# A hybrid encoder block on one core: gate and up of the first feed-forward column side by side, and half of the first norm's sum of squares on GpSimd

## Chip, core and metric

The kernel runs on one core of one Trainium2 chip. The metric is device time in microseconds of that core. The kernel before takes 1099.4 us, the median of 3 runs (1099.27 to 1099.45).

A core has engines with an instruction queue each: TensorE (PE in the profile; PEld are its weight loads), VectorE (DVE), ScalarE (ACT), GpSimd (POOL) and SyncE (SP), which issues the DMA transfers. They run side by side and wait for one another by semaphores.

## What is computed

One layer over 528 tokens (16 learned meta tokens and 512 of the input) with 1024 features, in float32:

```python
h = h + 0.5 * swiglu(rms_norm(h, ffn1_norm), ffn1_gate, ffn1_up, ffn1_down)
u = rms_norm(h, mix_norm)
proj = u @ w_in
y_attn = diff_attention_mixer(proj[..., :ATTN_COLS], ...)
y_rwkv = rwkv7_mixer(proj[..., ATTN_COLS:], ...)
h = h + concatenate([y_attn, y_rwkv]) @ w_out
h = h + 0.5 * swiglu(rms_norm(h, ffn2_norm), ffn2_gate, ffn2_up, ffn2_down)
return h[:, N_META:]

def swiglu(x, w_gate, w_up, w_down):
    return (silu(x @ w_gate) * (x @ w_up)) @ w_down

def rms_norm(x, g):
    return x * rsqrt(mean(x * x, axis=-1) + 1e-6) * g
```

The change concerns the first line alone, and of it the first microseconds. The feed-forward has 2816 inner features.

## The kernel before

**Tiles.** Activations are held transposed: features on the 128 partitions, tokens along the free axis. `hT` is eight tiles `h` of 128 features x 528 tokens, and the gate and up weights of one column of 128 inner features come as one tile of 128 x (8 x 128) each. A product over 528 tokens is done in two halves of 264, each in a PSUM bank (`mm`, 8 banks in all).

**Three products for one.** Each float32 operand is split into a high and a low part in the type fp32r: the high part by a copy on ScalarE, the low part by a subtraction on VectorE. A product is then hi x hi + lo x hi + hi x lo, three matmuls for each of the 8 feature tiles and each half (`mm3`). The high and low parts of the tokens are called `hh` and `hl` for the first six tiles, `sh` and `sl` for the last two (which lie in the room of weights that come later); those of the weights `whi` and `wlo`. The token's gain of the norm is applied in the split; the factor 1/rms, which is one number for each token, is applied to the finished products.

**The first feed-forward (`ffn`).** It has 22 columns in five groups (`FSPLIT`). The first four columns (`PLAIN`) are done with `plain`: gate product, then up product, each over all 8 feature tiles, so 2 x 48 matmuls. The others are done with `seven`, which needs combinations of the tokens (`xh`, `xl`, `th`, `tl`) that `operands` makes on VectorE and ScalarE; the weights of `seven` are loaded into the tiles `wr`, with parts `ws`, `sh`, `sl`, `uh`, `ul`. After a group of columns, its share of the output is added into `h` by `down`, whose products (with `whi`, `wlo` of the down weights) are spread between the columns of the next group.

**The norm.** `norm_add` squares one token tile on ScalarE (`fd`) and adds it on VectorE to the sum `fc`; `norm_end` sums over the partitions with a matmul against ones (`mm<-fc,ones`) and makes `r`, which is 1/rms. Every column's finished product waits for `r`, and so do the operands of `seven`.

**What sets the order.** All instructions are first recorded; `Recorder.flush` (line 255) then puts them into order with a list scheduler. It uses an estimated cost of each instruction (`cost_of`, line 84), the buffers that are free, and a priority `nc.prio`; of what is ready on an engine, the smallest priority goes first. So every instruction has the same line in the profile, L506, and tiles are told apart by name. The order written so is the order in each engine's queue. Priorities that matter here: the tokens' loads from `FIRST` = -20 in steps of 2, quarters of the first weight tile between them (`PIECES` = (4, 1): gate of column 0 in four quarters of 128 KB, up whole), the norm's squares and adds `NORM` = 1 (behind other work), `operands` 2, everything else 0. Before the first token arrives, nine warming matmuls on `ones` run.

Of the kernel before, what the change touches and what calls it, by code (L numbers as in the profile page):

```python
# [10 lines left out]
F32 = mybir.dt.float32  # L11
# [500 lines left out]
class Build:  # L512
    FSPLIT, HBUF = (5, 5, 4, 4, 4), 8
    WARM = 9
    INHB, LATE, NORM, UBUF = 6, 2, 1, 1
    PLAIN, SEVENS, RAWS = (4, 5), 4, 3
    EARLY = (2, 4)
    FIRST = -20
    PIECES = (4, 1)
    GROUPS = ((4, 5, 6, 7), (0, 1, 2, 3))  # L520
# [40 lines left out]

    def wtile(self, src, n, k=None, pieces=1, first=0):
        nc = self.nc
        raw = self.wraw.tile([128, 8, 128], F32, name="wraw")
        if pieces > 1:
            hi = self.whl.tile([128, 8, 128], F32R, name="whi")
            lo = self.whl.tile([128, 8, 128], F32R, name="wlo", bufs=2)
            m = n // pieces
            for o in range(0, n, m):
                s = slice(o, o + m)  # L570
                nc.prio = first + 2 * o if first else 0
                nc.sync.dma_start(raw[:, s], src[:, s])
                nc.prio = 0
                nc.scalar.activation(hi[:, s], raw[:, s], AF.Copy)
                nc.vector.tensor_tensor(lo[:, s], raw[:, s], hi[:, s].bitcast(F32), op=ALU.subtract)
            return hi, lo
        nc.sync.dma_start(raw[:, 0:n] if k is None else raw[:, 0:n].rearrange("p (d k) c -> p d k c", k=k), src)
        hi = self.whl.tile([128, 8, 128], F32R, name="whi")
        lo = self.whl.tile([128, 8, 128], F32R, name="wlo", bufs=2)
        nc.scalar.activation(hi[:, 0:n], raw[:, 0:n], AF.Copy)  # L580
        nc.vector.tensor_tensor(lo[:, 0:n], raw[:, 0:n], hi[:, 0:n].bitcast(F32), op=ALU.subtract)
        return hi, lo

    def mm3(self, w, n, x, out, at=0):

        nc = self.nc
        hi, lo = (t[:, at:at + n] for t in w)
        for i in range(n):
            for u, v in ((hi, 0), (hi, 1), (lo, 0)):
# [31 lines left out]
    def norm_add(self, st, src):  # L621
# [9 lines left out]
        nc.prio = prio  # L631

    def norm_end(self, st, psum, out):
        nc = self.nc
# [13 lines left out]

    def ffn(self, gu, dn, xs, n, st, h, done, pools, pieces=(1, 1)):

# [3 lines left out]
        parts = [(0, HALF), (HALF, HALF)] if n == L else [(0, n)]  # L654
        norm, r, gain = st
        self.norm_end(norm, psum, r)
        plain, before = self.PLAIN[n == MAIN], []
        f0 = 0
        for si, cnt in enumerate(self.FSPLIT):
            hs = []  # L660
            for i in range(cnt):
# [5 lines left out]
                if f < plain:  # L667
                    a = self.plain(gu, f, xs, r, n, parts, tp, pieces)
                else:
                    a = self.seven(gu, f, T, n, tp, sp, 3 if f < plain + self.LATE else 0)  # L670
# [19 lines left out]

    def plain(self, gu, f, xs, r, n, parts, tp, pieces):
        nc, psum = self.nc, self.pmm
        ps = []
        for g in range(2):
            w = self.wtile(gu[f, :, g], KT, pieces=1 if f else pieces[g], first=0 if f or g else self.FIRST + 1)
            pg = [psum.tile([128, 512], F32, name="mm") for _ in parts]
            self.mm3(w, KT, xs, [(o, m, p) for (o, m), p in zip(parts, pg)])
            ps.append(pg)
# [137 lines left out]
    def layer(self, ffn1=True, mixer=True, ffn2=True):  # L836
# [16 lines left out]
        with ExitStack() as ph:  # L853
# [16 lines left out]
            if ffn1:  # L870
# [3 lines left out]
                st = self.norm_begin(tp, L)  # L874
                for k in range(KT):
                    self.norm_add(st, hT[k])
                r1 = hp.tile([128, L], F32, name="r1")
                self.ffn(A["gu1"], A["dn1"], xs, L, (st, r1, lambda k: self.v("n1", k)), hT, done, (tp, hb, sp), self.PIECES)
# [741 lines left out]
```

## Time and profile before

| | before |
|---|---|
| median of 3 runs | 1099.4 us (1099.27 to 1099.45) |
| the profiled execution | 1091.92 us, its span 1090.1 us |
| TensorE busy | 1075.3 us, 99% of the span |
| VectorE busy | 834.7 us, 77% |
| ScalarE busy | 530.4 us, 49% |
| GpSimd busy | 10.1 us, 1%, 46 instructions |
| first token tile in use | matmuls on it from 5.29 us |
| TensorE without a gap | from 13.30 us for 96.75 us |

The span is the stretch from the first to the last recorded instruction of one profiled execution. A busy TensorE here is one that has a matmul in its pipeline; consecutive matmuls overlap, so the distance from one start to the next is shorter than the duration shown. The chain of waits follows the last instruction back to what released each step, and so shows which engine or transfer sets the end at each time. In a timeline row, `x2` means two instructions of the same kind, put together.

### The profile page before, as it was taken

The page shows a single profiled execution, that of the slowest core. Times are in us where ns is not written, and L with a number is a line of the kernel's source. Part 1 is how long each engine was busy: PE and PEld are TensorE (multiplying, and loading weights), DVE is VectorE, ACT ScalarE, POOL GpSimd, SP SyncE. Part 2 cuts the span into 40 slices and gives each one's busy share as a digit, 9 for nine tenths or more (in the row PEclk, how much of TensorE's full clock was granted, in tenths as well). Part 3 has the DMA queues.
Part 4 walks back from the last instruction along what each step waited for, and adds up shares of the span by engine and source line. Part 5 has one row for each costly group of instructions (what it writes and reads, how often), then busy time and mean ns, then how long its engine had stood idle before and what let it go on. Part 6 is the DMA issues. An engine that isn't in the chain of part 4 may idle for free.

```text
span 1090.1 us, 21488 instructions
## 1 busy us (share of the span) xinstructions
PE 1075.3 (99%) x8580; PEld 990.2 (91%) x8580; DVE 834.7 (77%) x1664; ACT 530.4 (49%) x945; POOL 10.1 (1%) x46
## 2 busy tenths in 40 slices
PE   8999999999999999999999999999999999999998
PEld 8999999999999998878888888688899999999996
DVE  7999786878875766887785657679978877777853
ACT  7554443433432654584576377646544443444421
POOL 0000000000000100000000000000000000000000
PEclk9999999999999999999999999999999999999999
DMA  7324324233221534434153222143233233233214
GB/s 241 116 63 134 106 72 127 72 103 113 76 64 46 193 116 110 115 99 115 51 140 80 69 80 78 59 156 121 96 93 108 91 107 112 68 116 117 68 30 135
DMA packets 75428, 110.57 MB, mean 101 GB/s; under 512 B 39488, under 2 KB 41024, under 8 KB 75328
## 3 DMA queue, kind: packets, MB, share of 16 engines
q1 hardware_dynamic: 75328, 109.19, 32.8%
q8 instruction: 68, 1.11, 0.4%
q14 instruction: 32, 0.26, 0.1%
HBM read 97.94 MB, written 10.04 MB: 99 GB/s over the span
## 4 chain that ended last, share of the span: by engine, by line
PE 89%; DVE 5%; ACT 2%; SPq 2%; DMA 1%; issue 1%; ACTq 0%; DVEq 0%
PE mm L506 89%; SPq L506 2%; DVE e L506 1%; DVE wlo L506 1%; DVE Tm L506 1%; DMA gd<-e 1%; DVE pr L506 1%; ACT e L506 0%; DMA h<-in_hT_dram 0%; DVE Zd L506 0%; DMA ad<-e 0%; ACT whi L506 0%; DVE n L506 0%; DVE xl L506 0%; DVE kb L506 0%
## 5 line engine op out<-in xcount | busy, mean ns | idle before, releaser
L506 ACT ACTIVATE whi<-wraw 128x1024 fp32r<-128x1024 f32 (+3 forms) x135 | 109.5, 811 | 167.2 <-PE mm L506 127.3
L506 PE MATMUL mm<-hh,wlo 128*128 128x264 f32 (+1 forms) x684 | 183.7, 322 | 1.3 <-DVE wlo L506 1.3
L506 PE MATMUL mm<-hl,whi 128*128 128x264 f32 (+1 forms) x684 | 184.3, 323 | 0.6 <-DVE hl L506 0.5
L506 PE MATMUL mm<-hh,whi 128*128 128x264 f32 (+1 forms) x684 | 184.2, 322 | 0.1
L506 PE MATMUL mm<-xl,sh 128*128 128x264 f32 (+1 forms) x490 | 138.5, 283 | 0.0
L506 PE MATMUL mm<-xh,sl 128*128 128x264 f32 (+1 forms) x490 | 138.5, 283 | 0.0
L506 PE MATMUL mm<-xh,sh 128*128 128x264 f32 (+1 forms) x490 | 138.1, 282 | 0.0
L506 ACT ACTIVATE sh<-ws 128x1024 fp32r<-128x1024 f32 x70 | 74.1, 1060 | 121.3 <-PE mm L506 116.2
L506 DVE TENSOR_TENSOR wlo<-wraw,whi 128x1024 fp32r<-128x1024 f32 (+3 forms) x135 | 122.7, 909 | 4.4 <-ACT whi L506 4.3
L506 PEld LDWEIGHTS mm<-hh,wlo 128*128 128x128 f32 x684 | 114.1, 189 | 11.0 <-DVE wlo L506 1.5
L506 PEld LDWEIGHTS mm<-hl,whi 128*128 128x128 f32 x684 | 114.3, 189 | 10.1 <-DVE hl L506 1.4
L506 PEld LDWEIGHTS mm<-hh,whi 128*128 128x128 f32 x684 | 114.4, 189 | 9.7 <-ACT hh L506 0.4
L506 PE MATMUL mm<-xh,whi 128*128 128x264 f32 (+1 forms) x448 | 114.4, 316 | 1.5 <-ACT whi L506 0.7
L506 PE MATMUL mm<-xh,wlo 128*128 128x264 f32 (+1 forms) x448 | 113.8, 315 | 1.4 <-DVE wlo L506 1.4
L506 PE MATMUL mm<-xl,whi 128*128 128x264 f32 (+1 forms) x448 | 112.5, 314 | 0.0
L506 PE MATMUL mm<-tl,sh 128*128 128x264 f32 (+1 forms) x350 | 99.0, 283 | 0.0
L506 PE MATMUL mm<-th,sl 128*128 128x264 f32 (+1 forms) x350 | 99.0, 283 | 0.0
L506 PE MATMUL mm<-th,sh 128*128 128x264 f32 (+1 forms) x350 | 98.9, 283 | 0.0
L506 DVE TENSOR_TENSOR sl<-ws,sh 128x1024 fp32r<-128x1024 f32 x70 | 85.5, 1222 | 16.4 <-ACT sh L506 16.4
L506 PEld LDWEIGHTS mm<-xh,sh 128*128 128x128 f32 x490 | 92.4, 189 | 0.8
L506 PEld LDWEIGHTS mm<-xl,sh 128*128 128x128 f32 x490 | 92.4, 189 | 0.7
L506 PEld LDWEIGHTS mm<-xh,sl 128*128 128x128 f32 x490 | 92.3, 188 | 0.0
(281 smaller groups left out, 2134.0 us busy)
## 6 DMA issues: line engine op xcount, KB each, us to landing
wr<-in_gu_dram SPq DMA_DIRECT2D x70, 512.0 KB, 4.1
wraw<-in_wi_dram SPq DMA_DIRECT2D x26, 512.0 KB, 3.6
wraw<-in_dn_dram SPq DMA_DIRECT2D x48, 256.0 KB, 2.7
wraw<-in_dn_dram SPq DMA_DIRECT2D x32, 320.0 KB, 3.0
wraw<-in_gu_dram SPq DMA_DIRECT2D x17, 512.0 KB, 3.7
wraw<-in_wo_dram SPq DMA_DIRECT2D x8, 512.0 KB, 4.0
h<-in_hT_dram SPq DMA_DIRECT2D x8, 264.0 KB, 4.9
h1d<-h SPq DMA_DIRECT2D x8, 264.0 KB, 2.1
```

The source lines that it names most:

```text
L506: ins = o.fn(*map(real, o.a), **{k: real(v) for k, v in o.k.items()})
```

## The change

The four constants: `PIECES` is 4 for (4, 1), and `NORM` -1 for 1. Three pieces of code:

- `begin` (new) issues the start of the first feed-forward. The gate and up weights of column 0 both come in four quarters, between the token tiles, and for each token tile the matmuls of gate and those of up follow each other. Behind them come the weights and products of the gate of column 1, whose weights (and those of its up) are put into the room of the weights of `seven` (`room=sp`).
- `norm_side` (new) squares the first four token tiles on GpSimd, each as a product of the tile with itself, and adds them up there: four products and three sums. VectorE and ScalarE do the other four tiles as before, and one more addition on VectorE takes GpSimd's sum `fb` into `fc`.
- `plain` uses what `begin` has made for columns 0 and 1.

With `NORM` at -1 the squares and adds of all three norms are ahead of work of priority 0, the two later norms' too.

```diff
-    INHB, LATE, NORM, UBUF = 6, 2, 1, 1
+    INHB, LATE, NORM, UBUF = 6, 2, -1, 1
-    PIECES = (4, 1)
+    PIECES = 4
...
-    def wtile(self, src, n, k=None, pieces=1, first=0):
+    def wtile(self, src, n, k=None, pieces=1, first=0, room=None):
         nc = self.nc
+        if room:
+            raw = room.tile([128, 8, 128], F32, name="wr", bufs=self.RAWS)
+            hi, lo = (room.tile([128, 8, 128], F32R, name=x) for x in ("sh", "sl"))
+            nc.sync.dma_start(raw, src)
+            nc.scalar.activation(hi, raw, AF.Copy)
+            nc.vector.tensor_tensor(lo, raw, hi.bitcast(F32), op=ALU.subtract)
+            return hi, lo
...
-    def mm3(self, w, n, x, out, at=0):
+    def mm3(self, w, n, x, out, at=0, only=None):
...
-        for i in range(n):
+        for i in range(n) if only is None else (only,):
...
+    def norm_side(self, pool, srcs):
+        nc = self.nc
+        acc = pool.tile(list(srcs[0].shape), F32, name="fb")
+        nc.gpsimd.tensor_tensor(acc, srcs[0], srcs[0], op=ALU.mult)
+        for x in srcs[1:]:
+            sq = pool.tile(list(x.shape), F32, name="fa")
+            nc.gpsimd.tensor_tensor(sq, x, x, op=ALU.mult)
+            nc.gpsimd.tensor_tensor(acc, acc, sq, op=ALU.add)
+        return acc
...
+        self.begun = {}
+        if pieces > 1:
+            self.begin(gu, xs, parts, sp, pieces)
         self.norm_end(norm, psum, r)
...
+    def begin(self, gu, xs, parts, sp, pieces):
+        ws = [self.wtile(gu[0, :, g], KT, pieces=pieces, first=self.FIRST + 1) for g in range(2)]
+        ps = [[self.pmm.tile([128, 512], F32, name="mm") for _ in parts] for _ in range(2)]
+        for i in range(KT):
+            for w, pg in zip(ws, ps):
+                self.mm3(w, KT, xs, [(o, m, p) for (o, m), p in zip(parts, pg)], only=i)
+        w = self.wtile(gu[1, :, 0], KT, room=sp)
+        pg = [self.pmm.tile([128, 512], F32, name="mm") for _ in parts]
+        self.mm3(w, KT, xs, [(o, m, p) for (o, m), p in zip(parts, pg)])
+        self.begun = {0: ps, 1: [pg]}
+
+    def plain(self, gu, f, xs, r, n, parts, tp, sp, pieces):
         nc, psum = self.nc, self.pmm
-        ps = []
-        for g in range(2):
-            w = self.wtile(gu[f, :, g], KT, pieces=1 if f else pieces[g], first=0 if f or g else self.FIRST + 1)
+        ps = self.begun.pop(f, [])
+        for g in range(len(ps), 2):
+            w = self.wtile(gu[f, :, g], KT, room=sp if f == 1 and pieces > 1 else None)
...
-                for k in range(KT):
+                side = self.norm_side(tp, hT[:4])
+                for k in range(4, KT):
                     self.norm_add(st, hT[k])
+                nc.prio = self.NORM
+                nc.vector.tensor_tensor(st["acc"], st["acc"], side, op=ALU.add)
+                nc.prio = 0
```

What moves in the order of the instructions, at the places that the prediction speaks of. First SyncE, the start of the program; `h` are token tiles, `wraw_105` the gate's and `wraw_106` the up's weights of column 0 (- before, + after):

```order
 L506 DMA h_94<-in_hT_dram 128x528
 L506 DMA wraw_105<-in_gu_dram 128x256
-L506 DMA h_109<-in_hT_dram 128x528
-L506 DMA h_112<-in_hT_dram 128x528
+L506 DMA wraw_106<-in_gu_dram 128x256
+L506 DMA h_111<-in_hT_dram 128x528
+L506 DMA h_115<-in_hT_dram 128x528
 L506 DMA wraw_105<-in_gu_dram 128x256
-L506 DMA h_118<-in_hT_dram 128x528
-L506 DMA h_130<-in_hT_dram 128x528
+L506 DMA wraw_106<-in_gu_dram 128x256
+L506 DMA h_134<-in_hT_dram 128x528
```

A quarter of up's weights now stands behind each quarter of gate's, ahead of token tiles that were ahead of it; before, up came whole behind the last token.

On GpSimd nothing stood here before. After the change its queue has this behind the constants' MEMSETs of the start; `fb_129` is its sum, `fa` a square:

```order
L506 ISA
L506 TENSOR_TENSOR fb_129<-h_94 128x528
L506 TENSOR_TENSOR fa_159<-h_111 128x528
L506 TENSOR_TENSOR fa_160<-h_115 128x528
L506 TENSOR_TENSOR fb_129<-fb_129,fa_159 128x528
L506 TENSOR_TENSOR fa_159<-h_134 128x528
L506 TENSOR_TENSOR fb_129<-fb_129,fa_160 128x528
L506 TENSOR_TENSOR fb_129<-fb_129,fa_159 128x528
```

The ISA row is an instruction that the compiler puts ahead of the first arithmetic of this kind on GpSimd.

On VectorE, behind the splits of the first tokens, before (rows 14 to 21 of its order); `fc_147<-fc_147,fd_185` is an add of the norm, `sl_217` the low part of the last token:

```order
L506 TENSOR_TENSOR fc_147<-fc_147,fd_185 128x528
L506 SCALAR_TENSOR_TENSOR sl_217<-h_169,vec_87,sh_208 128x528
L506 TENSOR_TENSOR wlo_155<-wraw_106,whi_135 128x1024
L506 TENSOR_TENSOR fc_147<-fc_147,fd_185 128x528
L506 TENSOR_TENSOR sl_218<-wr_178,sh_209 128x1024
L506 TENSOR_TENSOR fc_147<-fc_147,fd_185 128x528
L506 TENSOR_TENSOR sl_219<-wr_179,sh_210 128x1024
L506 TENSOR_TENSOR fc_147<-fc_147,fd_185 128x528
```

And after (rows 16 to 24), where `fc_207` is the norm's sum, `fb_129` GpSimd's, and `sl_271` and what follows are weights of column 1 and of `seven`:

```order
L506 SCALAR_TENSOR_TENSOR sl_270<-h_183,vec_87,sh_253 128x528
L506 TENSOR_TENSOR fc_207<-fc_207,fd_237 128x528
L506 SCALAR_TENSOR_TENSOR sl_270<-h_204,vec_87,sh_253 128x528
L506 TENSOR_TENSOR wlo_155<-wraw_105,whi_136 128x256
L506 TENSOR_TENSOR fc_207<-fc_207,fd_237 128x528
L506 TENSOR_TENSOR wlo_156<-wraw_106,whi_137 128x256
L506 TENSOR_TENSOR fc_207<-fc_207,fb_129 128x528
L506 TENSOR_TENSOR sl_271<-wr_214,sh_254 128x1024
L506 TENSOR_TENSOR sl_272<-wr_215,sh_255 128x1024
```

The adds of the norm now stand between the splits of the last tokens instead of behind them, there are fewer of them, and the last one, row 22, reads GpSimd's sum; all VectorE work of the later columns is behind it.

On TensorE, at the first matmul that reads the last operand `tl` (before: `tl_719`, row 440; rows 434 to 442 are shown):

```order
L506 MATMUL mm_102<-tl_717,sh_211 128x264
L506 MATMUL mm_102<-th_685,sl_220 128x264
L506 MATMUL mm_96<-xh_460,sh_208 128x264
L506 MATMUL mm_96<-xl_512,sh_208 128x264
L506 MATMUL mm_101<-xh_459,uh_264 128x264
L506 MATMUL mm_101<-xl_511,uh_264 128x264
L506 MATMUL mm_98<-tl_719,sh_210 128x264
L506 MATMUL mm_98<-th_687,sl_219 128x264
L506 MATMUL mm_101<-xh_459,ul_421 128x264
```

After, six matmuls of `down` (`hh_126` and `hh_127` with the down weights `whi_136`, `wlo_155`) stand at rows 437 to 442, between the products of the sevens:

```order
L506 MATMUL mm_103<-tl_783,uh_388 128x264
L506 MATMUL mm_96<-tl_784,sh_254 128x264
L506 MATMUL mm_96<-th_749,sl_271 128x264
L506 MATMUL mm_103<-th_748,ul_466 128x264
L506 MATMUL mm_97<-hh_126,whi_136 128x264
L506 MATMUL mm_97<-hl_145,whi_136 128x264
L506 MATMUL mm_97<-hh_126,wlo_155 128x264
L506 MATMUL mm_97<-hh_127,whi_136 128x264
L506 MATMUL mm_97<-hl_146,whi_136 128x264
L506 MATMUL mm_97<-hh_127,wlo_155 128x264
```

and the first matmul on the last operand, here `tl_787`, is row 471 (rows 467 to 472 are shown):

```order
L506 MATMUL mm_98<-th_751,sl_270 128x264
L506 MATMUL mm_100<-tl_785,sh_255 128x264
L506 MATMUL mm_100<-th_750,sl_272 128x264
L506 MATMUL mm_102<-xh_527,sl_270 128x264
L506 MATMUL mm_96<-tl_787,sh_254 128x264
L506 MATMUL mm_96<-th_752,sl_271 128x264
```

Up to that matmul TensorE's queue now has 31 more matmuls than before.

## Rows read from the trace of the kernel before

**Rows 1.** The page's first line of engines: busy us, share of the span, instructions

```profile
PE 1075.3 (99%) x8580; PEld 990.2 (91%) x8580; DVE 834.7 (77%) x1664; ACT 530.4 (49%) x945; POOL 10.1 (1%) x46
```

**Rows 2.** Chain that ended last, 0 to 110 us: start us, us, what

```profile
3.54 5.04 DMA h<-in_hT_dram
...
9.37 0.57 DVE hl L506
...
12.91 0.35 DVE wlo L506
...
13.30 96.75 PE mm L506 x771
```

**Rows 3.** Windows: stretch, length, busy (PE, PEld, DVE, ACT, POOL), clock, DMA, GB/s

```profile
0.00:20.00 20.00, 16.87 (x88) 15.11 (x89) 13.86 (x24) 15.77 (x25) 0.20 (x4) 0.91 0.86 294
...
80.00:100.00 20.00, 20.00 (x166) 20.00 (x165) 19.63 (x34) 10.93 (x16) 0.00 (x0) 1.00 0.32 108
sum 100.00, PE 96.87 PEld 94.57 DVE 93.32 ACT 59.53 POOL 0.20; mean PE 19.37 PEld 18.91 DVE 18.66 ACT 11.91 POOL 0.04
...
13.60:17.05 3.45, 3.45 (x18) 3.45 (x17) 3.45 (x5) 3.02 (x4) 0.00 (x0) 0.51 1.01 411
```

**Rows 4.** In time, at 66 us: start us, us, engine, line, operation, out<-in

```profile
65.11 0.70 DVE L506 TENSOR_TENSOR tl<-fb,th 128x528 fp32r<-128x528 f32 x1
...
66.00 0.28 PE L506 MATMUL mm<-tl,sh 128*128 128x264 f32 x1
```

**Rows 5.** In time on PE, in the first column, after it, norm sum

```profile
13.65 0.64 PE L506 MATMUL mm<-hh,whi 128*128 128x264 f32 x2
...
14.09 0.64 PE L506 MATMUL mm<-hl,whi 128*128 128x264 f32 x2
...
22.98 0.41 PE L506 MATMUL mm<-sh,wlo 128*128 128x264 f32 x2
...
23.22 0.41 PE L506 MATMUL mm<-hh,whi 128*128 128x264 f32 x2
...
24.45 1.16 PE L506 MATMUL mm<-fc,ones 128*128 128x264 f32 x4
```

**Rows 6.** In time: a DMA's issue on SP, the last token on ACT

```profile
1.64 0.43 SPq L506 DMA_DIRECT2D wraw<-in_gu_dram  x1
...
12.80 0.72 ACT L506 ACTIVATE sh<-h,vec 128x528 fp32r<-128x528 f32 x1
```

**Rows 7.** In time on DVE: splits, adds and sums of each shape

```profile
4.78 0.77 DVE L506 SCALAR_TENSOR_TENSOR hl<-h,vec,hh 128x528 fp32r<-128x528 f32 x1 [3.69 <-ACT hh L506]
...
12.83 0.76 DVE L506 TENSOR_TENSOR wlo<-wraw,whi 128x256 fp32r<-128x256 f32 x2
...
22.48 0.69 DVE L506 TENSOR_TENSOR ws<-ws,wr 128x512 f32<-128x512 f32 x1
...
24.31 1.22 DVE L506 TENSOR_TENSOR wlo<-wraw,whi 128x1024 fp32r<-128x1024 f32 x1
...
40.56 0.70 DVE L506 TENSOR_TENSOR xl<-fd,xh 128x528 fp32r<-128x528 f32 x1
41.17 0.70 DVE L506 TENSOR_TENSOR xl<-fb,xh 128x528 fp32r<-128x528 f32 x1
```

**Rows 8.** Groups on POOL by shape: busy us, mean ns, idle before

```profile
L506 POOL MEMSET O<- 128x1024 f32 x2 | 1.9, 957 | 12.7 <-PE mm L506 12.7
...
L506 POOL MEMSET vm<- 128x128 f32 x4 | 0.8, 205 | 475.5 <-PE mm L506 475.5
```

**Rows 9.** In time: the two COPYs on POOL and DVE beside them

```profile
385.56 0.76 DVE L506 SCALAR_TENSOR_TENSOR e<-praw,vec,e 128x528 f32<-128x528 f32 x1
...
385.95 0.42 POOL L506 COPY Mz<-eye 64x16 f32<-64x16 f32 x1 [4.62 <-DMA eye<-in_eye_dram]
...
471.40 1.22 DVE L506 TENSOR_TENSOR wlo<-wraw,whi 128x1024 fp32r<-128x1024 f32 x1
...
472.48 0.19 POOL L506 COPY Mz<-eye 64x16 f32<-64x16 f32 x1 [5.47 <-DMA zm<-Mz]
```

More of the change, by code (lines that the diff above doesn't have):

```diff
@@ L646, in norm_end, with ffn @@
             nc.vector.scalar_tensor_tensor(y, t, -3.0, y, op0=ALU.add, op1=ALU.mult)
-    def ffn(self, gu, dn, xs, n, st, h, done, pools, pieces=(1, 1)):
+    def ffn(self, gu, dn, xs, n, st, h, done, pools, pieces=1):
         nc, psum = self.nc, self.pmm
@@ L667, in ffn @@
                 if f < plain:
-                    a = self.plain(gu, f, xs, r, n, parts, tp, pieces)
+                    a = self.plain(gu, f, xs, r, n, parts, tp, sp, pieces)
                 else:
@@ L689, in down @@
             done(d)
-    def plain(self, gu, f, xs, r, n, parts, tp, pieces):
+    def begin(self, gu, xs, parts, sp, pieces):
[9 more added lines that the diff above has]
+    def plain(self, gu, f, xs, r, n, parts, tp, sp, pieces):
         nc, psum = self.nc, self.pmm
-        ps = []
-        for g in range(2):
-            w = self.wtile(gu[f, :, g], KT, pieces=1 if f else pieces[g], first=0 if f or g else self.FIRST + 1)
+        ps = self.begun.pop(f, [])
+        for g in range(len(ps), 2):
+            w = self.wtile(gu[f, :, g], KT, room=sp if f == 1 and pieces > 1 else None)
             pg = [psum.tile([128, 512], F32, name="mm") for _ in parts]
```

## Prediction

> **What bounds the kernel now.** I read the page first, then the chain of waits, then the windows of the first 120 us, and last the order in time on each engine around the places that these point to. TensorE is busy for 99% of the span, VectorE for 77%, GpSimd for 1% [rows 1]: whatever makes TensorE late or early by a microsecond moves the end by that microsecond. The chain shows where it is not yet so: up to 13.30 us it runs through the loads of the token tiles and their splits, and from there 96.75 us long through matmuls alone [rows 2]. The start of the first feed-forward is therefore the only place that this change can win at. The windows show the second thing: from 20 to 100 us TensorE is busy all the time, but VectorE too (93.32 of 100 us, and at least 19.63 of each 20 us from 20 on) [rows 3]. Its work is a chain of its own: the last operand of the first seven-product column (`tl`, of `operands`) starts on VectorE at 65.11 and takes 0.70, and the matmul that reads it starts at 66.00, 0.19 later [rows 4]. So at 66 us there is no slack between the two engines. A TensorE that is earlier is worth something only if VectorE is at 66 us not later.
>
> **What the change gives TensorE.** Before, only the gate product can run while the tokens come in; up runs after it and ends at 23.2 [rows 5]. After, both run on each token tile, 12 matmuls a tile. The four added DMAs bring up's 512 KB ahead of the last token instead of behind it. At the 294 GB/s of the first 20 us [rows 3] that is 1.8 us, and the last token's high half, at 12.80 before [rows 6], begins at about 14.5. SP issues them between others, 0.43 us each [rows 6], and nothing but these loads stands behind them. The split then needs 0.72 on ScalarE and 0.76 on VectorE [rows 6, 7], so 16.0; one add and two splits of weight quarters follow (0.62 + 2 x 0.35): 17.3. With the last eight matmuls TensorE has both products at about 18.3, against 23.2: 4.9 us ahead. A pair of matmuls takes 0.24 [rows 5], so 0.122 each.
>
> **What it asks of VectorE.** I count instructions in the order up to the last `tl`, and price them by the distance from one start to the next, which in a full queue is some 0.08 below the duration: 0.62 for 128x528 with two tensors, 0.68 with a gain, 0.35 for 128x256 (a pair of them takes 0.76), 0.61 for 128x512, 1.14 for 128x1024 [rows 7]. Before there are 104. After there are 106: four more of 128x256 (+1.4), three fewer adds of the norm (-1.9), one more of 128x512 (+0.6). So 58.7 us before and 58.8 after: no relief. What counts is when VectorE is through with the start, which ends with the new add of GpSimd's sum (`fc += fb`, row 22 of its order). I call its end T. Up to there VectorE has 8 x 0.68 + 8 x 0.35 + 4 x 0.62 = 10.8 us of work from 4.78 [rows 7] on. With the waits for the tokens it is through at T = 18.0 if GpSimd costs nothing: the 17.3 above and the add. That holds 18.0 - 4.8 - 10.8 = 2.4 us of waits. From T to the end of the last `tl` there are 86 instructions, 48.1 us, and 0.3 of small waits as before: T + 48.4.
>
> **The sum.** At the last `tl` the order of TensorE stands 31 matmuls further on than before (row 471 against 440), because matmuls of `down` fill in: 31 x 0.122 = 3.8 us of work already done. Before, that place is at 66.0; after, it is at T + 48.4 + 0.2. So the change of the time is T + 48.6 - 66.0 - 3.8 = **T - 21.2**. With T = 18.0 that is -3.2. (TensorE itself, from 18.3 through 370 matmuls at 0.122 and two halves of the norm's sum at 0.58 [rows 5], would be there at 64.6, so VectorE decides, and 1.7 us of the 4.9 are lost there.) What remains after it is the same work on both engines. At two earlier points I looked for a cost and found cover: TensorE runs at 1.2 GHz from 13.6 to 17.05 after idling [rows 3]; a pair there takes 0.44 [rows 5], so if it happens again TensorE loses at most 3.45 / 2 = 1.7 us, which the 2.0 us by which it waits at the last `tl` hold. The weights of the second column go to the room of the seven-product weights, whose next loads come later; their splits are in the count of 106. The earlier priority of the two later norms (-1 for 1) moves ScalarE and VectorE work where TensorE is busy and VectorE is not full: nothing.
>
> **What GpSimd does to T.** It gets seven instructions of 128x528, four squares and three sums, each with two inputs in SBUF. The trace has none of that kind, so I bound one from its MEMSETs and COPYs [rows 8]: 205 ns for 128 columns and 957 for 1024 make 0.84 ns a column and pass. One pass over 528 is 0.54 us; a fixed part of the shorter COPY (0.19) with two passes is 1.08, with three 1.52. I take 1.2, just above the two passes that two inputs need, so 8.4 us in all (3.8 to 10.6).
>
> Whether these run beside VectorE decides the case. The one thing the trace shows: a COPY of 64x16 on GpSimd takes 0.19 us at 472.48, where VectorE's big subtraction is just ending. The same COPY takes 0.42 at 385.95, where VectorE is in the middle of a 128x528 instruction with two SBUF tensors (385.56 + 0.76 = 386.32), and it ends at 386.37, right behind it [rows 9]. The reader on GpSimd seems to have been held until VectorE's instruction was over. In the start nearly all of VectorE's work is of this form. If the two take turns, T is moved by GpSimd's 8.4 us less what falls into VectorE's 2.4 us of waits. I take half of them, 1.2, since the tokens that end VectorE's waits start GpSimd as well: T = 18.0 + 8.4 - 1.2 = 25.2, and **+4.0 us: 1103.4**. It does not matter which one holds the other: what GpSimd has not done when VectorE reaches the add, VectorE waits for there. The ends are 3.8 - 2.4 (T = 19.4, -1.8) and 10.6 - 0 (T = 28.6, +7.4).
>
> The Trainium skill ("SBUF — State Buffer", section "Who interferes with whom") says the same as a rule, and it speaks against this change: a VectorE instruction with two SBUF inputs and a GpSimd instruction that reads SBUF exclude each other for the whole instruction, and the one issued second is blocked. The COPY of 0.42 us agrees. By the rule T is 25.2, without it 18.0.
>
> The Trainium skill ("GPSIMD Engine Reference", section "Elementwise — side-by-side cycle accounting") gives 4497 ns for such an addition of 2048 columns; scaled to 528 an estimate is 1.16 us, which would make the sum 1103.1. No run here shows it yet.
>
> **The rivals.**
> *Side by side.* GpSimd takes its sums from arrival to arrival and never holds VectorE; its last one ends before 17.3. Then T = 18.0 and the time is 1099.4 - 3.2 = 1096.2. For it: before, the fourth token was being split at 9.37 [rows 2]; with three weight quarters more ahead of it that is about 10.7, and the square and the sum that follow end at 13.1. Against it: the COPY of 0.42. It decides from T below 21.2 on.
> *Side by side, but late.* The order puts one more instruction, an ISA, on GpSimd ahead of its first square; the trace of before has no such row, so it may cost nothing or many microseconds. If the first square starts at s, GpSimd ends at s + 8.4 and T = s + 9.0. Break-even is s = 12.2; s between 10 and 14.4 makes -2.2 to +2.2, around 1099.4. Against it: GpSimd is busy for 0.20 of the first 20 us [rows 3], so the load would have to last 10 us.
> The Trainium skill ("GPSIMD Engine Reference", section "Instruction dispatch") gives about 6 us for the first call of a freshly loaded kernel. From 0.7 this would be s = 6.7, and T would still be 18.0; it would also take GpSimd out of VectorE's early waits, where the two take turns.
>
> **How the numbers follow.** Taking turns 0.58, side by side 0.24, side by side but late 0.18. The likeliest gives 1103.4, by itself 1100 to 1106.5. The sums are shifts against the profiled execution (1091.92, span 1090.1), which stands 7.5 below the median of the runs, 1099.4; I add them to the median. What a measurement of this kernel tells from no change is about 0.2%, 2.2 us, so 1097.2 and 1101.6 are the borders. Of the 0.58, 0.53 is above 1101.6, 0.04 between, 0.01 below; of the 0.24, 0.21 below and 0.03 between; of the 0.18, 0.13 between, 0.03 above, 0.02 below. Faster 0.24, same 0.20, slower 0.56. The range goes from 1096.2, the middle of the side by side case, to 1106.0; about 0.12 and 0.05 are left outside.
>
> **What would show it.** In the profile after: VectorE instructions of 128x528 and 128x256 between 5 and 25 us that are longer than 0.70 and 0.42, or idle ahead of them that ends with GpSimd; GpSimd instructions well over 1.2 us; `fc<-fc,fb` ending near 25 and waiting for GpSimd; the last `tl` near 73 and a wait of TensorE for it. I am wrong if `fc<-fc,fb` ends before 21: then the rest of the sum gives a gain. The sum itself is wrong if T is as I say and the last `tl` is not 48.4 behind it, or if a new wait of TensorE shows up after 75 us.

## Result, and the profile after

| | before | after |
|---|---|---|
| median of 5 runs | 1099.27 us (1097.7 to 1099.45) | 1104.62 us (1103.78 to 1105.47) |
| ratio | | 1.0052, 95% interval 1.0037 to 1.0066 |
| matmuls in the first 200 us of the profiled execution | 1558 | 1514 |
| end of the last `tl` | 65.81 us | 74.07 us |

The kernel became 5.35 us slower; the forecast was 1103.4, by taking turns. The two profiled executions, 1091.92 and 1105.47 us, are not subtracted here: most runs of the kernel before take 1098 to 1102 us and a few 1091 to 1093, at a granted clock that late in the span is a little higher, and the profiled one is such a run. So times are compared by medians, and the start by the number of matmuls done in the first 200 us, at 0.122 us each.

The profile after, first the windows of the profiled execution (stretch; length, busy us and count of PE, PEld, DVE, ACT, POOL; granted clock; DMA share; GB/s). They answer to [rows 3]; 22.38 is where the prediction's T now lies:

```profile
0.00:20.00 20.00, 15.37 (x92) 13.48 (x92) 13.80 (x20) 11.25 (x22) 9.80 (x11) 1.00 0.72 242
20.00:40.00 20.00, 18.18 (x133) 17.70 (x132) 17.95 (x30) 12.76 (x18) 0.00 (x0) 0.91 0.54 173
...
60.00:80.00 20.00, 19.29 (x151) 18.49 (x151) 20.00 (x39) 10.86 (x18) 0.00 (x0) 1.00 0.10 31
80.00:100.00 20.00, 19.76 (x161) 19.51 (x160) 18.60 (x34) 8.91 (x15) 0.00 (x0) 1.00 0.37 122
0.00:200.00 200.00, 192.59 (x1514) 189.18 (x1515) 170.69 (x294) 95.48 (x147) 9.80 (x11) 0.99 0.37 117
0.00:22.38 22.38, 17.75 (x110) 15.79 (x111) 16.18 (x25) 13.63 (x25) 9.80 (x11) 1.00 0.66 221
22.38:74.07 51.69, 49.16 (x379) 48.06 (x378) 48.74 (x87) 27.35 (x43) 0.00 (x0) 0.97 0.33 106
32.00:36.00 4.00, 4.00 (x22) 4.00 (x22) 4.00 (x10) 1.65 (x5) 0.00 (x0) 0.59 0.19 69
```

And of the kernel before the same view of the first 200 us:

```profile
0.00:200.00 200.00, 196.87 (x1558) 194.57 (x1559) 172.14 (x302) 100.41 (x152) 0.20 (x4) 0.99 0.37 118
```

After 200 us TensorE is 44 matmuls behind; 44 x 0.122 = 5.4 us. That agrees with the whole loss, so the loss lies in the start; from 200 to 700 us TensorE is idle for 7.6 us, against 7.9 before, so nothing later needs to be explained. The count is a rough measure all the same: in e8, below, it gives 5.4 us too where the ratio of the times gives 3.6. TensorE has done more than before at 20 us (92 against 88 [rows 3]), loses most between 20 and 40 (133 against 161), and still loses from 60 to 100 (309 against 328), where VectorE is busy for 38.60 of the 40 us.

GpSimd's instructions (six of the seven), in time (start us, us, engine, line, operation, out<-in; in brackets the idle time before and what ended it):

```profile
4.10 1.07 POOL L506 TENSOR_TENSOR fb<-h 128x528 f32<-128x528 f32 x1 [3.66 <-DMA h<-in_hT_dram]
7.26 2.56 POOL L506 TENSOR_TENSOR fa<-h 128x528 f32<-128x528 f32 x2 [2.10 <-DMA h<-in_hT_dram]
9.78 1.77 POOL L506 TENSOR_TENSOR fb<-fb,fa 128x528 f32<-128x528 f32 x1
...
12.72 3.23 POOL L506 TENSOR_TENSOR fb<-fb,fa 128x528 f32<-128x528 f32 x2
```

Beside them VectorE, in the same view, and the wait and the two ends that the sum turns on:

```profile
7.99 2.40 DVE L506 SCALAR_TENSOR_TENSOR hl<-h,vec,hh 128x528 fp32r<-128x528 f32 x2 [1.59 <-ACT hh L506]
10.31 2.74 DVE L506 TENSOR_TENSOR wlo<-wraw,whi 128x256 fp32r<-128x256 f32 x2
12.97 3.55 DVE L506 SCALAR_TENSOR_TENSOR hl<-h,vec,hh 128x528 fp32r<-128x528 f32 x2
16.44 0.75 DVE L506 TENSOR_TENSOR wlo<-wraw,whi 128x256 fp32r<-128x256 f32 x2
...
21.68 0.70 DVE L506 TENSOR_TENSOR fc<-fc,fb 128x528 f32<-128x528 f32 x1
...
29.20 0.43 DVE L506 SCALAR_TENSOR_TENSOR r<-fc,r 128x264 f32<-128x264 f32 x1
30.66 0.69 DVE L506 TENSOR_TENSOR ws<-wr 128x512 f32<-128x512 f32 x1 [1.03 <-DMA wr<-in_gu_dram]
...
73.37 0.70 DVE L506 TENSOR_TENSOR tl<-fb,th 128x528 fp32r<-128x528 f32 x1
```

While GpSimd computes, a pair of 128x256 takes 2.74 us; the next pair, with GpSimd done at 15.95, takes 0.75, the 0.76 of before [rows 7]. That is the lengthening that the prediction named as its sign. T is 21.68 + 0.70 = 22.38, though, not near 25.

Last TensorE, in the same view:

```profile
31.75 0.39 PE L506 MATMUL mm<-hh,sh 128*128 128x264 f32 x1 [1.82 <-DVE fa L506]
...
32.72 0.64 PE L506 MATMUL mm<-hl,sh 128*128 128x264 f32 x2
...
74.33 0.28 PE L506 MATMUL mm<-tl,sh 128*128 128x264 f32 x1
```

The last row is the matmul that reads the last operand, 0.26 us behind it, at 66.00 before [rows 4]. And the chain that ended last (start us, us, what):

```profile
24.68 5.96 DMA wr<-in_gu_dram
...
31.27 0.44 DVE fa L506
31.75 19.09 PE mm L506 x142
50.86 0.77 DVE fb L506 x2
...
71.08 1.15 DVE sl L506
72.27 15.56 PE mm L506 x124
...
91.27 1.14 DVE sl L506
92.46 37.63 PE mm L506 x306
```

Before, the chain ran through matmuls alone from 13.30 on. The 96.75 us of [rows 2] end where that view's window ends, at 110 us (and the last row here at 130); in the chain of the whole span the stretch is 379.52 us long, to 392.82. Now the chain is on VectorE from 50.86 to 72.27 and again at 91.27. Ahead of that is a wait that the prediction did not have: at 31.75 TensorE has stood for 1.82 us until VectorE's `fa<-mm,r` read a finished product out of its PSUM bank. The factor `r` was there at 29.63, but the read stood in VectorE's queue behind `ws<-wr`, which waited for its load until 30.66. After this standstill its matmuls take 0.64 a pair in place of 0.41, and the granted clock of 32 to 36 us is 0.59: for a good part of that stretch it is at the lower level, 1.2 GHz.

### The profile page after: what moved, and what is told of

Its sections match the earlier page's. It is cut to its first block, busy times and chain, and to the rows that moved or that the text cites. A ratio compares the mean times of both kernels' runs of the same rounds, so it can differ in the third digit from the quotient of the medians.

```text
span 1103.4 us, 21521 instructions
## 1 busy us (share of the span) xinstructions
PE 1084.4 (98%) x8580; PEld 994.6 (90%) x8580; DVE 838.6 (76%) x1664; ACT 528.6 (48%) x944; POOL 19.9 (2%) x53
## 4 chain that ended last, share of the span: by engine, by line
PE 81%; DVE 10%; ACT 3%; DMA 3%; issue 2%; SPq 1%; ACTq 0%; DVEq 0%
PE mm L506 81%; DVE e L506 2%; DVE wlo L506 1%; SPq L506 1%; DMA gd<-e 1%; DVE kb L506 1%; DVE n L506 1%; DVE Tm L506 1%; DMA wr<-in_gu_dram 1%; ACT e L506 1%; DMA ad<-e 1%; DVE pr L506 0%; ACT whi L506 0%; DMA h<-in_hT_dram 0%; DVE xl L506 0%
## 5 line engine op out<-in xcount | busy, mean ns | idle before, releaser
L506 ACT ACTIVATE whi<-wraw 128x512 fp32r<-128x512 f32 (+3 forms) x136 | 107.5, 793 | 165.6 <-PE mm L506 125.7
L506 PE MATMUL mm<-hl,whi 128*128 128x264 f32 (+1 forms) x660 | 179.4, 323 | 1.4 <-DVE hl L506 1.3
L506 PE MATMUL mm<-hh,whi 128*128 128x264 f32 (+1 forms) x660 | 179.3, 323 | 1.0 <-ACT hh L506 1.0
L506 PE MATMUL mm<-hh,wlo 128*128 128x264 f32 (+1 forms) x660 | 179.1, 323 | 1.2 <-DVE wlo L506 1.2
L506 DVE TENSOR_TENSOR wlo<-wraw,whi 128x512 fp32r<-128x512 f32 (+3 forms) x136 | 122.9, 905 | 5.1 <-ACT whi L506 4.9
L506 PEld LDWEIGHTS mm<-hl,whi 128*128 128x128 f32 x660 | 110.2, 188 | 11.2 <-DVE hl L506 2.4
L506 PEld LDWEIGHTS mm<-hh,wlo 128*128 128x128 f32 x660 | 110.2, 188 | 11.0 <-DVE wlo L506 1.6
L506 PEld LDWEIGHTS mm<-hh,whi 128*128 128x128 f32 x660 | 110.5, 188 | 10.3 <-ACT hh L506 1.2
```

Source lines behind the costliest of these rows:

```text
L506: ins = o.fn(*map(real, o.a), **{k: real(v) for k, v in o.k.items()})
```

## Experiments

Ratios are against runs of the kernel before on the same chip; e1 to e4, e5 to e8 and e9 to e12 shared a chip. The expectations name the theories themselves; in short, the forecast's is that VectorE and GpSimd take turns at SBUF, and against it stand that only the waiting for GpSimd's sum costs, that the new order itself costs, and that VectorE's full queue decides whatever TensorE waits for.

### e1: GpSimd's part for 32 of the 528 tokens

```diff
+        s = slice(0, 32)
-        nc.gpsimd.tensor_tensor(acc, srcs[0], srcs[0], op=ALU.mult)
+        nc.gpsimd.tensor_tensor(acc[:, s], srcs[0][:, s], srcs[0][:, s], op=ALU.mult)
...
+        nc.gpsimd.memset(acc[:, 32:], 0.0)
```

The other squares and sums are cut alike, and all other queues are the same.

> The changed kernel, but GpSimd squares and adds up only the first 32 of the 528 tokens (the rest of its sum is set to zero, so half of the norm's squares is left out for 496 tokens); the order on every other engine is the same, instruction for instruction. Theory A, turns: VectorE and GpSimd hold each other up, so with seven short instructions the long VectorE rows (pairs of 2.4, 2.7 and 3.5 us between 8 and 16.5) go back to 0.7 each, fc<-fc,fb ends near 18.0 instead of 22.4, and the time is 1096 to 1098. Theory B, begin itself: the moved loads, the weights of column 1 in the sevens' room and the new order cost the 5 us, GpSimd's work beside it nothing: fc<-fc,fb ends not before 21 and the time is 1103 to 1106.

Measured: 1099.69 us, ratio 1.0008 (0.9984 to 1.0031). The windows of e1, up to its T, from there to the end of its last `tl`, and of the first 200 us:

```profile
0.00:18.29 18.29, 16.70 (x110) 15.68 (x111) 11.46 (x24) 12.59 (x23) 3.42 (x12) 1.00 0.82 262
18.29:68.76 50.47, 48.33 (x379) 46.67 (x378) 48.81 (x87) 28.38 (x45) 0.00 (x0) 1.00 0.35 111
...
0.00:200.00 200.00, 196.04 (x1559) 192.99 (x1560) 171.41 (x302) 98.42 (x151) 3.42 (x12) 1.00 0.38 118
```

T is 18.29 and VectorE's work up to it 11.46 us in place of 16.18. So GpSimd's work costs T 4.1 us and the kernel about 4.9 (1104.62 - 1099.69; by the ratios 0.44%, 4.8). But without it the new order gains nothing: 1559 matmuls at 200 us against 1558 before.

### e2: e1 with seven full instructions on GpSimd that nobody reads

```diff
+        nc.prio, d = 5, self.rm
+        for i, x in enumerate(srcs):
+            nc.gpsimd.tensor_tensor(d, x, x, op=ALU.mult)
+            if i:
+                nc.gpsimd.tensor_tensor(d, d, x, op=ALU.add)
+        nc.prio = 0
```

> As the run with 32 tokens, and GpSimd does seven 128x528 instructions on the same four tokens besides, into a tile that nobody reads before it is overwritten 200 us later. So no engine waits for that work. Theory A, turns: VectorE's rows are stretched by 4 to 5 us in sum all the same, fc<-fc,fb ends at 21 to 23, the time is 1102 to 1105. Rival, the wait alone: VectorE loses time only because it waits for GpSimd's sum; then VectorE's rows are 0.7 each and the time is that of the run with 32 tokens, 1096 to 1098.

Measured: 1105.16 us, ratio 1.0052 (1.0035 to 1.007), T 23.18. VectorE in e2, in time:

```profile
14.92 1.82 DVE L506 TENSOR_TENSOR fc<-fc,fd 128x528 f32<-128x528 f32 x1
16.66 1.57 DVE L506 SCALAR_TENSOR_TENSOR hl<-h,vec,hh 128x528 fp32r<-128x528 f32 x1
18.15 1.83 DVE L506 SCALAR_TENSOR_TENSOR sl<-h,vec,sh 128x528 fp32r<-128x528 f32 x1
19.90 0.70 DVE L506 TENSOR_TENSOR fc<-fc,fd 128x528 f32<-128x528 f32 x1
```

No instruction on another engine needs the added results, GpSimd's sum itself is done at 14.71 us, and the whole loss is back. It is contention, not a wait for the sum.

### e3: the new order without GpSimd's part, the norm at -1

```diff
-                side = self.norm_side(tp, hT[:4])
-                for k in range(4, KT):
+                for k in range(KT):
                     self.norm_add(st, hT[k])
-                nc.prio = self.NORM
-                nc.vector.tensor_tensor(st["acc"], st["acc"], side, op=ALU.add)
-                nc.prio = 0
```

> The changed kernel with all eight squares on ScalarE and all seven adds on VectorE (NORM -1 kept), nothing of it on GpSimd. Theory A: three adds more on VectorE, 1.9 us, no turns: the last add ends at 18 to 20, T - 21.2 gives -3 to -1, so 1096 to 1098.5. Theory B: the 5 us stay, 1103 to 1106.

Measured: 1104.17 us, ratio 1.0048 (1.0032 to 1.0065). The expectation was missed, by a cause that it didn't hold. TensorE in e3:

```profile
15.06 0.81 PE L506 MATMUL mm<-hh,whi 128*128 128x264 f32 x2 [2.57 <-ACT whi L506]
```

With eight squares on ScalarE at a priority ahead of the splits, the weights' high parts come late: 68 matmuls in the first 20 us against 92. So this run doesn't price the new order; e7 does.

### e4: the preparation of the sevens' weights behind the first products' multiplications by r

```diff
...
+            late = [o for o in order[at:to + 1] if o.eng in ("vector", "scalar")
+                    and name(o) in ("ws", "uh", "sh", "sl", "ul")]
+            keep = [o for o in order[at:to + 1] if o not in late]
+            order[at:to + 1] = keep + late
```

`at` is the place behind the last `r` ahead of the first `ws`, `to` that of the sixth `fa` or `fb` behind it.

> The changed kernel with six instructions moved in two queues: the first split and sums of the first seven-product column's weights (uh, sh on ScalarE; ws, sl, ws, ws on VectorE) go behind the multiplications by r of the first two columns, instead of ahead of them. Theory C: VectorE's wait for the late load of wr (1.0 us at 29.6) held up fa<-mm,r, and through it TensorE (1.82 us idle to 31.75, and some 3.3 us at 1.2 GHz behind it): then the idle time and the low clock at 32 go and the time falls by 2 to 3.5, to 1101 to 1102.5. Rival D: VectorE decides again at 70 us anyway, its wait there grows by what was won, and the time stays at 1103.5 to 1105.5.

Measured: 1105.32 us, ratio 1.006 (1.0036 to 1.0084). The windows of e4:

```profile
20.00:40.00 20.00, 19.97 (x160) 19.50 (x159) 16.76 (x27) 12.99 (x18) 0.00 (x0) 1.00 0.48 159
40.00:60.00 20.00, 19.42 (x157) 19.04 (x157) 19.64 (x37) 9.60 (x16) 0.00 (x0) 1.00 0.28 86
60.00:80.00 20.00, 16.92 (x126) 15.64 (x125) 20.00 (x40) 10.54 (x18) 0.00 (x0) 1.00 0.12 34
```

The wait at 31.75 and the lower clock behind it are gone: 160 matmuls from 20 to 40 us against 133. From 40 to 80 they are 281 against 315, and the last `tl` starts at 74.26 against 73.37, since VectorE waited too: 2.24 us at 35.90 for `sh`, and 16.76 us of work from 20 to 40 in place of 17.95. What TensorE has ahead of VectorE it gives back. But the edit itself made VectorE 0.9 us later, so the run doesn't show that the wait at 31.75 costs nothing.

### e5: the kernel before, with GpSimd's part alone

```diff
+                side = self.norm_side(tp, hT[:4])
-                for k in range(KT):
+                for k in range(4, KT):
                     self.norm_add(st, hT[k])
+                nc.prio = self.NORM
+                nc.vector.tensor_tensor(st["acc"], st["acc"], side, op=ALU.add)
+                nc.prio = 0
```

(`norm_side` as in the change).

> The kernel before (gate first, then up, PIECES (4, 1), NORM 1), and only the norm moved: squares and sums of the first four tokens on GpSimd, the sum added on VectorE. Theory A, turns: between 5 and 17 us VectorE's rows are stretched by 3 to 5 us in sum, the splits of the last tokens are late by that, and three adds fewer (1.9 us) give some of it back: 1100.5 to 1103. Rival: GpSimd costs something only together with the new order of the loads: then three adds fewer show as 0 to -2, 1097 to 1099.5.

Measured: 1102.04 us, ratio 1.0027 (1.0015 to 1.0039), +3.0 us; T is 24.88. Its VectorE, in time:

```profile
10.42 1.53 DVE L506 TENSOR_TENSOR wlo<-wraw,whi 128x256 fp32r<-128x256 f32 x1
```

And its first window:

```profile
0.00:20.00 20.00, 15.17 (x62) 13.13 (x63) 13.36 (x18) 10.54 (x18) 10.09 (x11) 0.74 0.75 251
```

The part of the change on GpSimd loses by itself, in the old order too. Here it stretches the very splits that TensorE waits for: 62 matmuls at a clock of 0.74 against 88 [rows 3].

### e6: 16 tokens on GpSimd, and column 1's weights out of the sevens' room

```diff
-            raw = room.tile([128, 8, 128], F32, name="wr", bufs=self.RAWS)
-            nc.sync.dma_start(raw, src)
+            for s, x in ((slice(0, 4), "fa"), (slice(4, 8), "fb")):
+                raw = room[1].tile([128, 4, 128], F32, name=x)
+                nc.sync.dma_start(raw, src[:, s])
```

(the splits by halves likewise; `norm_side` with `slice(0, 16)`).

> As the run with 32 tokens on GpSimd (here 16, and VectorE adds only these 16 columns; the rest of the first four tokens' squares is left out), and the weights of column 1 are loaded into four tiles fa, fb that are idle until r is ready, not into the sevens' tiles wr, so that all three wr can be loaded behind the last token, as before the change. Theory R: the sum missed 4 us because the change takes two of three wr tiles until VectorE has split column 1, so that the sevens' weights land 10 us later and VectorE waits for them (0.67 at 25.6 and what follows): 1095.5 to 1097.5. Rival: VectorE's work behind 18 us is the bound whatever the loads do: 1098.5 to 1100.5, as with 32 tokens.

Measured: 1097.71 us, ratio 0.9989 (0.9971 to 1.0008), between the two forecasts, so it decides nothing. The room is free earlier, but the place where TensorE stands only moves; TensorE in e6:

```profile
28.82 0.39 PE L506 MATMUL mm<-hh,sh 128*128 128x264 f32 x1 [3.41 <-DVE fc L506]
```

### e7: e3 with the norm at 1, as before

```diff
-    INHB, LATE, NORM, UBUF = 6, 2, -1, 1
+    INHB, LATE, NORM, UBUF = 6, 2, 1, 1
```

> The changed kernel with the norm as before: all squares on ScalarE, all adds on VectorE, NORM 1. So of the change only the order of gate and up, the pieces and the room are left. Theory P: the run with everything on VectorE and NORM -1 was slow (1104.2) because squares and adds stood ahead of the splits; with NORM 1 they stand behind and the time is 1098 to 1101. Rival: 1.9 us more of adds and the wr tiles cost 5 us wherever they stand: 1103 to 1105.

Measured: 1100.06 us, ratio 1.0009 (0.999 to 1.0028). This is the new order alone, with the whole norm where it was: no change that can be told. It also shows what was wrong with e3: the same kernel with the norm at -1 is some 4.3 us slower (by the ratios, 1.0048 and 1.0009).

### e8: the norm's sum by matmuls in place of VectorE's adds

```diff
+                st["ps"] = [psum.tile([128, 512], F32, name="mm") for _ in range(2)]
+                for k in range(KT):
+                    sq = hb.tile([128, L], F32R, name=("hh", "hl")[k % 2])
+                    nc.scalar.activation(sq, hT[k], AF.Square)
+                    for i, p in enumerate(st["ps"]):
+                        nc.tensor.matmul(p[:, 0:HALF], self.onesr, sq[:, i * HALF:(i + 1) * HALF],
+                                         start=k == 0, stop=k == KT - 1)
...
```

`NORM` is 1 here too, and the rest of the first norm is at -2.

> The changed kernel without GpSimd and without adds: ScalarE squares all eight tokens (fp32r), TensorE sums them up by 16 matmuls against ones in two PSUM banks while the tokens arrive (1.95 us for 1.16), and the rest of the norm has priority -2. VectorE has no adds at all (4.3 us fewer than before), r is ready near 18 instead of 27 to 29, and the operands can start there. Theory V: VectorE is the bound up to 70 us, so its 4.3 us count: 1094.5 to 1097.5. Rival: TensorE has to wait for the wr tiles and the later splits of the weights' last quarters anyway: 1099 to 1102.

Measured: 1103.31 us, ratio 1.0033 (1.002 to 1.0047), a miss. It was to take the adds off VectorE, and put something else in the way on TensorE (its row in time):

```profile
13.15 0.81 PE L506 MATMUL mm<-hh,ones 128*128 128x264 f32 x2 [8.14 <-ACT hh L506]
```

A summing matmul stands in TensorE's queue ahead of the products of the first tokens and waits 8.14 us for its square. The run says nothing on what a VectorE with fewer adds is worth.

### e9 and e10: e1 with other work on GpSimd

The first piece is e9, the second e10; nobody reads what they write.

```diff
+        nc.prio = 5
+        for i in range(30):
+            nc.gpsimd.memset(self.rm, 0.0)
...
+        for x in srcs:
+            for i in range(2):
+                nc.gpsimd.tensor_copy(self.rm, x)
```

For e9:

> As the run with 32 tokens (the other 496 tokens' squares of four tiles left out; order of all other engines the same), and GpSimd runs 30 MEMSETs of 128x528 besides, some 13 us of work that reads nothing, into a tile that nobody reads then. Theory A, narrow: VectorE and GpSimd take turns where both read SBUF; a MEMSET reads nothing and holds nobody: VectorE's rows stay at 0.7 to 0.77, fc<-fc,fb ends at 18 to 19, 1098.5 to 1100.5. Rival, wide: any GpSimd instruction holds VectorE: the rows stretch as with the squares, fc<-fc,fb ends behind 20, 1101.5 to 1105.

For e10:

> As before, with eight COPYs of 128x528 on GpSimd (one input in SBUF each) in place of the MEMSETs, on the four tokens as they land. Theory A, one input is enough: the COPY of 64x16 that took 0.42 for 0.19 waited for VectorE, so these wait and hold too: VectorE's rows are stretched by 2 to 5 us in sum, fc<-fc,fb ends at 20 to 23, 1101 to 1105. Rival: only instructions with two SBUF inputs on GpSimd hold VectorE: 18 to 19, 1098.5 to 1100.5.

Measured: e9 1099.88 us, ratio 1.001 (1.0 to 1.002), T 18.31; e10 1102.36 us, ratio 1.0033 (1.0019 to 1.0048), T 20.08. GpSimd and VectorE of e9, in time:

```profile
11.27 12.52 POOL L506 MEMSET rm<- 128x528 f32 x21
...
13.04 0.70 DVE L506 TENSOR_TENSOR fc<-fc,fd 128x528 f32<-128x528 f32 x1
```

and of e10:

```profile
4.22 0.62 POOL L506 COPY rm<-h 128x528 f32<-128x528 f32 x1
...
12.98 3.96 POOL L506 COPY rm<-h 128x528 f32<-128x528 f32 x4
...
13.24 1.12 DVE L506 TENSOR_TENSOR fc<-fc,fd 128x528 f32<-128x528 f32 x1
14.29 1.12 DVE L506 SCALAR_TENSOR_TENSOR hl<-h,vec,hh 128x528 fp32r<-128x528 f32 x1
15.33 1.12 DVE L506 SCALAR_TENSOR_TENSOR sl<-h,vec,sh 128x528 fp32r<-128x528 f32 x1
16.38 1.12 DVE L506 TENSOR_TENSOR fc<-fc,fd 128x528 f32<-128x528 f32 x1
17.43 0.76 DVE L506 SCALAR_TENSOR_TENSOR sl<-h,vec,sh 128x528 fp32r<-128x528 f32 x1
```

From 13 to 17 us GpSimd is busy without a gap in both. Beside MEMSETs, which only write, VectorE's rows keep their 0.70. Beside COPYs, which read one tile, four rows in a row are 1.12 each, as many as there are COPYs in that stretch, and the fifth is 0.76. So it is GpSimd's reading that holds VectorE, and one read tile is enough. The Trainium skill ("SBUF — State Buffer", section "Who interferes with whom") makes the same distinction between a GpSimd instruction that reads SBUF and one that writes it only, and these two runs agree.

### e11: e1 with one load of the sevens' weights cut to an eighth

```diff
+            if self.flushes == 1 and o.dma is not None and o.a and o.a[0].tensor.name.split("_")[0] == "wr":
+                loads += 1
+                if loads == 4:
+                    o.a = tuple(x[:, 0:1] for x in o.a)
```

The rest of that tile keeps what was in it.

> As the run with 32 tokens, instruction for instruction, but the one load that VectorE waits for at 26.29 (the up weights of the first seven-product column, into a tile wr that column 1 has just left) moves an eighth, 64 KB, so the rest of that weight is wrong. Theory W: the sum missed this wait; the load now lands 2 to 3 us earlier, VectorE's 0.67 us of idle ahead of ws<-wr goes, TensorE's 1.36 us at 27.38 falls to 0.3 to 0.7, the last tl ends 0.7 to 1 us earlier than 68.76 and the time is 0.5 to 1 below that run: 1098.5 to 1099.3. Rival: VectorE's other work takes the place, the last tl ends at 68.5 to 68.9 and the time is the same.

Measured: 1099.77 us, ratio 1.0003 (0.9994 to 1.0013). The wait of VectorE for that load (0.67 us in e1) is gone, TensorE's wait for `fa` falls from 1.36 to 0.76, and the last `tl` starts at 67.55, half a microsecond earlier than in e1, which lies between the two forecasts. The time doesn't move measurably: by the ratios it is 0.5 us below e1, within both intervals, so the run doesn't decide between them.

### e12: what the runs point to, together

Column 1's weights come as in e6, the norm is without GpSimd as in e3, and besides:

```diff
+    INHB, LATE, NORM, UBUF = 6, 2, 1, 1
...
             nc.scalar.activation(sq, src, AF.Square)
+            nc.prio = 0
             nc.vector.tensor_tensor(st["acc"], st["acc"], sq, op=ALU.add)
...
+        nc.prio = -2
         self.norm_end(norm, psum, r)
+        nc.prio = 0
```

> A whole kernel without GpSimd work: gate and up of column 0 side by side as in the change; column 1's weights in the idle tiles fa, fb instead of wr; squares on ScalarE behind the splits (priority 1), adds on VectorE as they come (0), and the rest of the first norm at -2, so that r does not wait behind the sevens' preparation. All seven adds are on VectorE, so its work up to the last tl is that of before, but it starts 2 us earlier into the operands. I expect 1096.5 to 1098.5. Rival: VectorE is as full as before and gives nothing back: 1099 to 1100.5.

Measured: 1098.89 us, ratio 1.0007 (0.9993 to 1.0021). Its first 200 us:

```profile
0.00:200.00 200.00, 196.34 (x1575) 194.58 (x1576) 174.13 (x310) 101.40 (x157) 0.20 (x4) 1.00 0.37 121
```

It is 17 matmuls, 2.1 us, ahead of the kernel before at 200 us, and its time is not measurably another. Why the 2.1 us don't reach the end stays open; none of these kernels is shown to beat the kernel before.

## Why the prediction was right, and where its sizes were off

**The mechanism was right.** The case with the highest chance was that GpSimd's seven instructions and VectorE's take turns. e2 brings the loss back with work that nobody waits for, e5 shows it in the old order, e9 and e10 tell reading from writing. Of the signs that the prediction named, the longer VectorE rows came. Two others came that were to count against its sum, though T is not where it had put it: the last `tl` lies 51.69 us behind T instead of 48.4, and TensorE has a new wait after 75 us (0.24 us at 92.46, for VectorE's `sl`). The forecast of turns rested on a COPY of 0.42 us [rows 9], a single row, and the row of 0.19 us that it was compared with, at 472.48, lies partly inside a VectorE instruction too (up to 472.62); it carried.

**The sum came near by luck: its errors cancel.** It was T - 21.2.

| term | predicted | measured | effect on the sum |
|---|---|---|---|
| T without GpSimd | 18.0 | 18.29 (e1) | +0.3 |
| what GpSimd adds to T | 7.2 | 4.1 | -3.1 |
| VectorE's work, T to the last `tl` | 48.1 | 48.74 | +0.6 |
| its idle time there | 0.3 | 2.95 | +2.65 |
| matmuls ahead of the last operand | 31 more | 31 more in the queue (row 471 against 440) | 0 |
| last `tl` to 200 us | 0 | 5.4 - 4.5 | +0.9 |

From +4.0 these lead to 5.35. The last row is what the count at 200 us leaves over, and the count is rough, so it confirms little that the medians show the same. The prediction had put this row at nothing ("the same work on both engines"); of the 0.9 us, the wait at 92.46 shows 0.24, and the rest stays open.

The first mis-sized step is what GpSimd adds to T. A product takes 1.07 us where nearly nothing runs beside it (4.10); no sum runs alone, and if it takes as long, seven are 7.5, not 8.4. VectorE's work up to T grew by 16.18 - 11.46 = 4.7 us, so by this estimate 2.8 of the 7.5 fell into its waits for the tokens, where I had taken 1.2; and VectorE's remaining idle time up to T was 0.6 shorter than in e1.

The second is "T + 48.4", that VectorE would run on from T without a gap. It stood idle for 2.95 us. The largest piece, 1.03 us at 30.66, is a wait for a load of the sevens' weights, whose room column 1's weights now fill until VectorE has split them. The prediction had put that move down as free, because the loads "come later". The first of them starts at 24.68, and VectorE stands waiting when it has landed; in e11 a shorter load takes the same wait of e1 away.

**The cover that was named did not hold all of it.** I had looked for TensorE's waits at the token tiles alone, and had said that the 2.0 us by which it waits at the last `tl` would hold a loss. The wait that came, 1.82 us at 31.75 with the lower clock behind it, comes from products that are finished and occupy PSUM banks until VectorE multiplies them by `r`, and the late load above holds that multiplication up. In e4, with the wait gone, 27 matmuls are won by 40 us and 34 are lost by 80. That fits the claim that VectorE decides there, but does not show it for this wait, since e4 delays VectorE too.

**The rival "side by side" was too good.** With T at 18.29 the sum gives 18.29 - 21.2 = -2.9, hence 1096.5. e1 measured no change. From T to the last `tl` it took 50.47 (48.81 of work, 1.66 idle) in place of 48.4, which leaves -0.8 there, and by 200 us that is gone too. The lead of TensorE, 21 matmuls or 2.6 us at 60 us (432 against 411), has shrunk to 6 at 80 and to 1 at 100. From 60 to 100 us VectorE is busy for 38.66 of 40 us, and TensorE's waits there are for VectorE's `xl` (0.44 us at 65.48) and `sl` (0.23 at 87.08) and for ScalarE's `th` (0.17 at 66.50). So the new order alone is worth nothing that can be measured (e1, e7), and the GpSimd part costs nearly all of the 5 us.

**The late first call didn't occur.** The first square starts at 4.10, when its token has landed. The Trainium skill ("GPSIMD Engine Reference", section "Instruction dispatch") gives about 6 us for the first call of a freshly loaded kernel, which would be 6.7 here; this trace doesn't show it. A delay of up to the 3.66 us that GpSimd stood idle ahead of its token would not show. For the size, the estimate of 1.16 from its section "Elementwise — side-by-side cycle accounting" stands beside the measured 1.07.

## What to carry to other kernels

An idle engine is not free room: before moving work to it, look in the trace for an instruction of its own that reads the same memory beside the busy engine, and price the move by how much the busy one's rows get longer. When one engine is early, count work and idle time of the other full engine up to the place where they meet; a lead is worth only what that queue lets through, and finished products that wait for a factor hold their PSUM banks meanwhile. A tile borrowed from a later stage delays that stage's loads until it is read, even where those seem to come much later; what this cost in time no run here settles (e6, e11).

## What the runs showed of the hardware that was not expected

- VectorE and GpSimd give way to one another instruction by instruction: beside four COPYs of 128x528 four VectorE rows of 0.70 to 0.76 became 1.12 (e10); beside instructions with two inputs they became 1.5 to 1.8 (e2).
- MEMSETs on GpSimd, 12.52 us of them on end, left VectorE as it was (e9).
- The first arithmetic on GpSimd started at the landing of its input (4.10 us); no delay of its own showed beyond the 3.66 us of idle time before it.
- TensorE's granted clock fell to 0.59 of full speed over 32 to 36 us after a standstill of 1.82 us (after); with the standstill removed, 20 to 40 us ran at 1.00 (e4). The length of the standstill alone doesn't tell: behind one of 1.84 us at 29.48 the clock fell to 0.74 over 32 to 36 us (e10), behind one of 1.84 us at 27.52 it stayed at 1.00 up to 40 (e12).
